# A gate projection as seven products of halves: layer 1 of a hybrid decoder trunk on one Trainium2 core

## The chip, the core and the metric

The kernel runs on one core of a Trainium2 chip. The core has TensorE (PE, matmuls; its weight loads are listed as PEld), VectorE (DVE), ScalarE (ACT), GpSimd (POOL) and SyncE (SP, which here only issues transfers). The metric is the device time of one run in microseconds; lower is better. Before the change the median of three runs is 888.65 us (888.0 to 889.33).

## The reference

Two layers over x of 1024 tokens and 1024 features, all in float32. Layer 0 is sliding-window attention, layer 1 a gated linear recurrence (HGRN2). Both end with a gate z, an output projection, a norm and a residual. The change touches layer 1 and the end of layer 0:

```python
def hgrn2_mixer(h, lower_bound, w_in, gnorm_w, w_out):
    proj = h @ w_in                                   # 1024 x 4096
    q, f, i, z = jnp.split(proj, [1024, 2048, 3072], axis=-1)
    q = silu(q); log_f = ...; k = -expm1(log_f); v = i   # 8 heads, key and value width 128
    o = chunked_gated_recurrence(q, k, v, log_f)      # S_new = S * decay + k^T v, head by head
    o = o * rsqrt(mean(o * o) + eps) * gnorm_w
    o = o.reshape(B, T, 1024) * silu(z)
    return o @ w_out

for layer in range(2):
    h = rmsnorm(x, pre_norm_w[layer])
    y = mixer(h)
    x = x + rmsnorm(y, post_norm_w[layer])
```

The gate projection z = h @ W_z is a product of 1024x1024 by 1024x1024.

## The kernel before

**Products.** float32 operands are split into a high and a low part (float32r): the high part is a rounded copy, the low part the difference. `product` (L230) then issues three matmuls of 128x512 for one block: high by high, high by low, low by high. Weights come as a stream of 128x512 entries, 256 KB each (list `SRC`). `fetch` issues their transfers on SP into four raw slots in turn (L151); for each entry `advance` issues a high split on ScalarE (L187) and a low split on VectorE (L188) into one of ten pairs of buffers (`whi`, `wlo`). An entry is split when a pair is free, and a raw slot is fetched again when its low split is done. Activations lie transposed and split in `act[k, half]` (k the eight blocks of 128 features, half the tokens 0 to 511 or 512 to 1023).

**Layer 0's end.** `output0` runs the output projection of layer 0, the norms and the residual row by row, and for each half of the tokens transposes the normed rows into `act[k, half]` (`transpose_half`, L289; high part on ScalarE at L212, low part on VectorE at L218).

**Layer 1.** `mixer1` runs a list of units, `plan`: units of i (value projection, columns 0 to 511 as c = 0 and 512 to 1023 as c = 1), of q and f (`qf`, one head), and `rec(h)`, the recurrence of head h. In `rec`, VectorE prepares two scans U and V (L973, L974) and products of them, TensorE makes the scores (psd L1004, pss L1014, psq L1030), transposes the keys (pst L1047), ScalarE copies them to `yn` (L1048), TensorE forms the chunks' updates (psk L1053), VectorE chains the state S through seven chunks (L1057, L1059), and TensorE reads it for the output (pso L1066, L1068), which is normed into `vo` (L1074). `yn` and `S` have one buffer each. Between the units of i stand four rounds of `weight_sums` (L1087 to L1090), each of which loads four blocks of the output projection's weights into the buffers of `yn` and `S`, forms sums of quarters there on VectorE and stores them to DRAM (`td`).

The gate z is 16 units of 24 matmuls (eight feature blocks by three): two of them ahead of `rec(7)`, six after, eight in `final1`. Each is evicted by a Sigmoid on ScalarE (L1106), a product on VectorE (L1107) and a product with the recurrence's output on GpSimd (L1108). `final1` then has the output projection in seven products of quarter matrices in place of eight (Strassen's scheme in Winograd's form): each takes four row blocks of 12 matmuls, and reads sums of quarters of both operands.

**The order.** The instructions of each engine have a fixed order, made when the kernel is built: a scheduler places units that the code gives with priorities (`hp()` raises the splits) and marks (`keep_in_program_order`). An engine takes its instructions one after the other, so one that waits holds those behind it. The program holds two variants of the network and chooses by the data; the runs here take the first.

Of the kernel before, what the change touches and what calls it, by code (L numbers as in the profile page):

```python
# [23 lines left out]
P = 128  # L24
# [66 lines left out]
def emit(tc, I, out):  # L91
# [9 lines left out]
    with top:  # L101
# [10 lines left out]
        td = [dp.tile([4 * P, 512], F32, name=f"td{i}") for i in range(4)]  # L112
# [23 lines left out]
        B1 = 116  # L136
        SRC = [I["w"][i] for i in range(B1)]
        quarter = lambda q: [I["w"][B1 + 4 * q + k] for k in range(4)]
        sums_of = lambda i: [td[i][k * P:(k + 1) * P, :] for k in range(4)]
        SRC += quarter(0) + sums_of(0) + sums_of(1) + sums_of(2) + sums_of(3) + quarter(3) + quarter(1)  # L140
# [144 lines left out]
        def transpose_half(hns, half, scol, then={}):  # L285
            for k in range(NK):
# [3 lines left out]
                ins = act_from_psum(k, half, pt, cst[:, scol + k:scol + k + 1])  # L290
# [549 lines left out]
        def output0(o, fp):  # L840
# [21 lines left out]
            def norm(t):  # L862
                xn = xns.pop(t)
                hn = fp.tile([P, D], F32, tag="hn", bufs=5, name="hn")
                jk = fp.tile([P, D], F32, tag="jkx", name="jkx")
# [16 lines left out]
        def mixer1(fast, vo, rp):  # L882
# [8 lines left out]
            nb3 = 3 if fast else 2  # L891
# [187 lines left out]
            zu = [lambda t=t: z_unit(rp, vo, 0, t) for t in range(8)]  # L1079

            def weight_sums(k):
# [3 lines left out]
                for q, x in enumerate((b11, b21, b12, b22)):  # L1085
                    nc.sync.dma_start(x, I["w"][B1 + 4 * q + k])
                v.tensor_tensor(b22, b22, b12, op=ALU.subtract)  # L1087
# [22 lines left out]
        def final1(vo, fp):  # L1110


            wpost = fp.tile([P, D], F32, name="wpost1")
            nc.sync.dma_start(wpost, I["bc"][2:3, :].to_broadcast([P, D]))
            ssall = fp.tile([P, 2, 9], F32, name="ssall")

            af = {(k, 0): fp.tile([P, 512], F32, name=f"af{k}") for k in range(NK)}
            af.update({(k, 1): vo[k // 4][:, k % 4, :] for k in range(NK)})
            late = [vo[k // 4][:, 4 + k % 4, :] for k in range(NK)]
            s3 = late[:4]  # L1120
            s2p = [(fp.tile([P, 512], F32R, name=f"s2h{k}"), fp.tile([P, 512], F32R, name=f"s2l{k}")) for k in range(4)]
            p1 = [fp.tile([P, 512], F32, name=f"p1_{t}") for t in range(4)]
            u3 = [fp.tile([P, 512], F32, name=f"u3_{t}") for t in range(4)]
# [14 lines left out]
            def part(ps, left, e, t, more, done=True, cols=(0, 512)):  # L1138

                c = slice(t * P, (t + 1) * P)  # L1140
                for k in range(4):
                    hi, lo = left[k]
                    product(ps, k, (hi[:, c], lo[:, c]), weight(e, k, *cols), None if more else 0, 3)
                    if done:
                        used(e + k)

            def row_part(c, t, y, x, cs, ss):

                jk = fp.tile([P, 512], F32, tag="sg", bufs=2, name="jk")
                nc.scalar.activation(jk[:, :cs.stop - cs.start], y, AF.Square, scale=D ** -0.5, accum_out=ss)  # L1150
# [229 lines left out]
```

## Time and profile before

| | |
|---|---|
| median of three runs | 888.65 us (888.0 to 889.33) |
| the profiled execution: its time, its span | 888.05 us, 886.3 us |
| granted TensorE clock | 0.998 |
| busy: PE, DVE, ACT, POOL | 98%, 68%, 48%, 38% |
| matmul records | 5214 |
| stage of layer 0's last transposes | about 360 to 402 us |
| sums of the output projection's weights | 402 to 437 us |
| z, with rec(7) in it | 690 to 800 us |
| out projection | to 878 us |

The page's section 1 gives busy time and share of each engine, section 4 the chain of work that ended last. The timeline gives start, duration, engine, line and operation of single instructions, with the idle time before them and what ended it in brackets. The windows give the busy time of each engine in a stretch, then clock, DMA share and GB/s. The list of waits gives for each line what it waited for: us in total, times, longest.

### The profile page before, as it was taken

To read this page: it belongs to the slowest core of one execution; us is meant where nothing else is said; L and a number is where in the kernel's file an instruction comes from. 1 tells how busy PE (TensorE), PEld (TensorE's weight loads), DVE (VectorE), ACT (ScalarE), POOL (GpSimd) and SP (SyncE) were. 2 spreads that over 40 slices of the span, in tenths; PEclk is the share of its full clock that TensorE was granted. 3 is DMA by queue.
4 is the path that set the end of the run, shared out by engine and by line. 5 is a ranking of instruction groups with operands and counts; after the bars stand their busy time and mean duration, and the time that the engine had idled before them with its cause. 6 is when DMAs were issued, how large, how long until landed. Compare 5 with 4: busy or idle time off the path is not lost.

```text
span 886.3 us, 14409 instructions
## 1 busy us (share of the span) xinstructions
PE 867.1 (98%) x5214; PEld 721.1 (81%) x5214; DVE 604.0 (68%) x975; ACT 426.9 (48%) x1094; POOL 333.0 (38%) x491
## 2 busy tenths in 40 slices
PE   6999999999999999999999999999999999999996
PEld 5887888888888878878888888888888788888885
DVE  6998887677899436764568775137668844448985
ACT  5735777767688332542323341343343333447432
POOL 4543644655666303320054342115243533220032
PEclk9999999999999999999999999999999999999999
DMA  9766455313232134555711010021111001503434
GB/s 339 274 204 176 145 167 154 92 50 96 58 92 85 48 89 149 170 177 192 264 51 40 27 49 1 20 89 36 48 50 36 13 1 51 187 1 107 131 123 167
DMA packets 61977, 94.17 MB, mean 106 GB/s; under 512 B 5832, under 2 KB 25928, under 8 KB 61896
## 3 DMA queue, kind: packets, MB, share of 16 engines
q1 hardware_dynamic: 61616, 93.08, 33.3%
q8 instruction: 43, 0.70, 0.3%
q14 instruction: 38, 0.31, 0.1%
q10 hardware_dynamic: 280, 0.07, 0.0%
HBM read 70.22 MB, written 21.07 MB: 103 GB/s over the span
## 4 chain that ended last, share of the span: by engine, by line
PE 81%; DVE 7%; issue 4%; POOL 3%; ACT 2%; DMA 2%; DVEq 0%; POOLq 0%; ACTq 0%
PE psmm L230 47%; PE psmm L88 20%; PE pss L88 3%; PE pso L88 2%; POOL rstd L269 2%; PE psk L1053 1%; PE pst L88 1%; PE pso L1066 1%; PE pso L1068 1%; POOL ms L267 1%; PE pst L1047 1%; PE pst L1134 1%; PE psd L1004 1%; DMA qd<-qh 1%; DMA out_dram<-xr 1%
## 5 line engine op out<-in xcount | busy, mean ns | idle before, releaser
L230 PE MATMUL psmm<-whi,acth 128*128 128x512 f32 x448 | 176.3, 395 | 1.1 <-DVE y L832 1.1
L230 PE MATMUL psmm<-wlo,acth 128*128 128x512 f32 x448 | 175.0, 391 | 0.0
L230 PE MATMUL psmm<-whi,actl 128*128 128x512 f32 x448 | 174.9, 392 | 0.0
L188 DVE TENSOR_TENSOR wlo<-wraw,whi 128x512 fp32r<-128x512 f32 x132 | 96.3, 742 | 71.2 <-ACT whi L187 67.5
L187 ACT ACTIVATE whi<-wraw 128x512 fp32r<-128x512 f32 x124 | 77.5, 631 | 94.9 <-PE psmm L230 72.6
L88 PE MATMUL psmm<-acth,whi 128*128 128x512 f32 x272 | 110.5, 406 | 1.7 <-ACT whi L88 1.7
L88 PE MATMUL psmm<-actl,whi 128*128 128x512 f32 x272 | 107.3, 394 | 0.2 <-DVE actl L88 0.2
L88 PE MATMUL psmm<-acth,wlo 128*128 128x512 f32 x272 | 107.4, 395 | 0.0
L230 PE MATMUL psmm<-acth,whi 128*128 128x512 f32 x256 | 101.1, 395 | 0.2 <-DVE qf L906 0.2
L230 PE MATMUL psmm<-acth,wlo 128*128 128x512 f32 x256 | 100.4, 392 | 0.0
L230 PE MATMUL psmm<-actl,whi 128*128 128x512 f32 x256 | 100.3, 392 | 0.0
L230 PEld LDWEIGHTS psmm<-whi,acth 128*128 128x128 f32 x448 | 84.1, 188 | 19.1 <-DVE y L832 1.9
L230 PEld LDWEIGHTS psmm<-whi,actl 128*128 128x128 f32 x448 | 84.1, 188 | 17.2
L230 PEld LDWEIGHTS psmm<-wlo,acth 128*128 128x128 f32 x448 | 84.2, 188 | 16.7
L717 ACT ACTIVATE sm<-sm,st 128x129 f32<-128x129 f32 x128 | 49.9, 393 | 26.6 <-DVE st L715 26.5
L914 POOL TENSOR_SCALAR gate<-gate,lbt 128x512 f32<-128x512 f32 x16 | 17.8, 1109 | 118.9 <-ACT gate L912 108.4
L88 PEld LDWEIGHTS psmm<-acth,wlo 128*128 128x128 f32 x272 | 51.6, 190 | 11.7 <-DVE wlo L88 0.2
L88 PEld LDWEIGHTS psmm<-acth,whi 128*128 128x128 f32 x272 | 51.8, 191 | 10.3 <-ACT whi L88 2.0
L88 PEld LDWEIGHTS psmm<-actl,whi 128*128 128x128 f32 x272 | 51.8, 190 | 8.6 <-DVE actl L88 0.7
L230 PEld LDWEIGHTS psmm<-acth,whi 128*128 128x128 f32 x256 | 48.1, 188 | 10.8 <-DVE qf L906 0.9
L230 PEld LDWEIGHTS psmm<-acth,wlo 128*128 128x128 f32 x256 | 48.1, 188 | 10.1
L230 PEld LDWEIGHTS psmm<-actl,whi 128*128 128x128 f32 x256 | 48.1, 188 | 9.4
(312 smaller groups left out, 1727.4 us busy)
## 6 DMA issues: line engine op xcount, KB each, us to landing
wraw<-in_w SPq DMA_DIRECT2D x128, 256.0 KB
QS<-qd SPq DMA_DIRECT2D x16, 512.0 KB
xr<-in_x SPq DMA_DIRECT2D x8, 512.0 KB
x1d<-xn SPq DMA_DIRECT2D x8, 512.0 KB
bq<-in_w SPq DMA_DIRECT2D x16, 256.0 KB
td<-bq SPq DMA_DIRECT2D x16, 256.0 KB
wraw<-td SPq DMA_DIRECT2D x16, 256.0 KB
xr<-x1d SPq DMA_DIRECT2D x8, 512.0 KB
```

What stands on the lines that cost most here:

```text
L88: return (lambda *a, **k: self.tc.keep_in_program_order(f(*a, **k))) if self.on else f
L187: nc.scalar.activation(hi, raw, AF.Copy)
L188: W["split_ins"][i] = v.tensor_tensor(lo, raw, hi.bitcast(F32), op=ALU.subtract)
L230: W["mm"] = pe.matmul(ps, a, b, start=(k == first and i == 0), stop=(k == last and i == 2), skip_group_check=first is None)
L267: keep(g.tensor_scalar(m, ms, eps, 1.0, op0=ALU.add, op1=ALU.mult))
L269: W["rstd"] = keep(g.tensor_tensor(r, m, nhalf[:, :width], op=ALU.pow))
L717: W["exp"] = nc.scalar.activation(sm[:, h, :], sm[:, h, :], AF.Exp, bias=nm[:, h:h + 1], scale=-1.0, accum_out=dn[:, h:h + 1])
L914: nc.gpsimd.tensor_scalar(dst, dst, ol, lb, op0=ALU.mult, op1=ALU.add)
L1004: nc.tensor.matmul(ps[o:o + 32, c, :], V[:, cs], U[:, cs], start=True, stop=True)
L1047: nc.tensor.transpose(pt[:, i, :], Y[:, c * P:(c + 1) * P], ident)
L1053: nc.tensor.matmul(pk[:, i, :], yn[:, c, :], vt[:, c, hc], start=True, stop=True)
L1066: nc.tensor.matmul(po[:, i, :], sc[:, c, :], vt[:, c, hc], start=True, stop=(c == 0))
```

## The change

The gate projection of layer 1 is written as seven products of halves too (z1 to z7), so that both it and the output projection are. In numbers of matmuls, z goes from 16 x 24 = 384 to 7 x 4 x 12 = 336.

- The **sums of the inputs** (`zS1` to `zS4`, four sums of quarters of the normed, transposed activations) are formed in `output0` while the transposes lie in PSUM: 12 copies on ScalarE and 16 operations on VectorE more, and 16 stores of 256 KB to DRAM (`sd`). Later they come back as entries of the weight stream and are split into the buffers `act[k, half]` themselves. `INTO` says into which, and a counter `W["phase"]`, raised by `next_phase()`, holds the stream until the old contents have been read by the program.
- The **sums of the weights** are four more rounds of `weight_sums`, with its own quarters (`QZ`) and signs, between the units of i with c = 1; they go to DRAM (`tz`).
- The stream has 44 entries of 256 KB for z in place of 16 (28 of weights and weight sums, 16 of input sums).
- Of z's products, three row blocks of z1 stand ahead of `rec(7)`; the rest is in `final1` in the order z1, z7, z6, z4, z5, z3, z2. Their results are added on VectorE in SBUF, Silu on ScalarE is applied to the sum (in place of Sigmoid and a product), and GpSimd multiplies as before.
- The out projection's products come in another order of quarters (o1, o7, o6, o4, o5, o3, o2), and the pool of the recurrence stays open to the end; `final1` takes its buffers by name from those of the recurrence. Four buffers for the residual's rows in place of five.

```diff
+        for e in (("z1", QZ[0]), ("zS3", sd[0], (1, 1)), ("z7", tz[0]), ("zS2", sd[1], (0, 2)), ("z6", tz[1]), ("z4", tz[2]),
+                  ("zS1", sd[2], (1, 3)), ("z5", tz[3]), ("zS4", sd[3], (0, 4)), ("z3", QZ[3]), ("z2", QZ[2]),
+                  ("o1", QO[0]), ("o7", td[0]), ("o6", td[1]), ("o4", td[2]), ("o5", td[3]), ("o3", QO[3]), ("o2", QO[2])):
+            entries(*e)
...
+                elif i in INTO:
+                    k, half, phase = INTO[i]
+                    if W["phase"] < phase:
+                        return
+                    W["place"][i] = act[k, half]
...
+            def sums(k, half, pt, scale):
+                a1, a2 = vo1[:, k % 4, :], vo1[:, 4 + k % 4, :]
+                r = slice(k % 4 * P, k % 4 * P + P)
+                if half == 0:
+                    nc.scalar.activation(a1 if k < 4 else a2, pt, AF.Copy, scale=scale)
+                elif k < 4:
+                    a21[k] = fp.tile([P, 512], F32, tag="a21", bufs=2, name="a21")
+                    nc.scalar.activation(a21[k], pt, AF.Copy, scale=scale)
+                    v.tensor_tensor(a1, a21[k], a1, op=ALU.subtract)
+                    nc.sync.dma_start(sd[0][r], a1)
+                else:
+                    s2, s1 = fp.tile([P, 512], F32, tag="s2", bufs=2, name="s2"), a21[k - 4]
+                    v.scalar_tensor_tensor(s2, pt, scale, a1, op0=ALU.mult, op1=ALU.add)
+                    v.scalar_tensor_tensor(s1, pt, scale, s1, op0=ALU.mult, op1=ALU.add)
+                    v.tensor_tensor(a2, a2, s2, op=ALU.subtract)
+                    for d, x in ((1, s2), (2, s1), (3, a2)):
+                        nc.sync.dma_start(sd[d][r], x)
...
-            plan += qf(0) + ([zeros] if fast else []) + qf(1) + rc(0) + qf(2) + rc(1) + qf(3) + rc(2) + iu(1) + rc(3)
-            plan += qf(4) + qf(5) + rc(4) + qf(6) + rc(5) + qf(7) + rc(6) + zu[:2] + rc(7) + zu[2:]
+            def first_parts():
+                next_phase()
+                for t in range(3):
+                    first_part(t, p1z[t])
...
+            plan = ... rc(2) + with_sums(iu(1), QZ, tz, True) + rc(3)
+            plan += qf(4) + qf(5) + rc(4) + qf(6) + rc(5) + qf(7) + rc(6) + [first_parts] + rc(7)
...
-        def z_unit(pool, vo, c, t):
-            ps = proj_nat(100 + 8 * c, t)
-            sg = pool.tile([P, 512], F32, tag="sg", bufs=2, name="sg")
-            nc.scalar.activation(sg, ps, AF.Sigmoid)
-            v.tensor_tensor(sg, ps, sg, op=ALU.mult)
-            nc.gpsimd.tensor_tensor(vo[c][:, t, :], vo[c][:, t, :], sg, op=ALU.mult)
+            def gate(c, t, z):
+                nc.scalar.activation(z, z, AF.Silu)
+                nc.gpsimd.tensor_tensor(vo[c][:, t, :], vo[c][:, t, :], z, op=ALU.mult)
...
+            first_part(3, p1z[3])
+            next_phase()
+            for t in range(4):
+                ps = mm()
+                part(ps, quad(0, 1), "z7", t, False)
+                nc.scalar.activation(u3[t], ps, AF.Copy)
+            next_phase()
+            for t in range(4):
+                ps = mm()
+                part(ps, quad(0, 0), "z6", t, False)
+                v.tensor_tensor(p1[t], ps, p1z[t], op=ALU.add)
+                v.tensor_tensor(u3[t], u3[t], p1[t], op=ALU.add)
+            next_phase()
+            for t in range(4):
+                ps = mm(tag="to"[t % 2])
+                part(ps, quad(4, 1), "z4", t, False)
+                sg = sgs[t % 2]
+                v.tensor_tensor(sg, ps, u3[t], op=ALU.add)
+                gate(0, 4 + t, sg)
...
```

The line numbers from here on with another range are those of the changed kernel: its splits are L203 and L204, the copy of yn is L1088, the steps of S are L1097 and L1099, and the copy of F is L1009.

**ScalarE, around rec(6)'s copy of yn.** `sg` are z's sigmoids, `sc0` and `sc1` the masked scores of rec(6) and rec(7), `pst` the transposed keys. Before:

```order
L1106 ACTIVATE sg_6967<-psmm_6942 128x512 [waits DVE_49,PE_49]
L1033 ACTIVATE sc0_4153<-psq_6847 64x4x64 [waits PE_49]
L1033 ACTIVATE sc0_4153<-psq_6847 64x4x64
L1106 ACTIVATE sg_6996<-psmm_6971 128x512 [waits DVE_49,PE_49]
L1048 ACTIVATE yn_6868<-pst_6870 128x512 [waits PE_49]
L1048 ACTIVATE yn_6868<-pst_6885 128x512 [waits PE_49]
L1017 ACTIVATE sc1_4154<-pss_7058 32x4x32 [waits PE_49]
```

After (`acth0_0` to `acth3_0` take the sum zS2, `whi4` to `whi7` the weights of z6, `pair` are results of z1 and z7):

```order
L1073 ACTIVATE sc0_4219<-psq_6951 64x4x64
L203 ACTIVATE acth0_0_116<-wraw0_112 128x512 [waits DMAHW6_49,PE_49]
L203 ACTIVATE acth1_0_120<-wraw1_113 128x512 [waits DMAHW7_49,PE_49]
L203 ACTIVATE acth2_0_124<-wraw2_114 128x512 [waits DMAHW0_49,PE_49]
L203 ACTIVATE acth3_0_128<-wraw3_115 128x512 [waits DMAHW1_49,PE_49]
L1175 ACTIVATE pair_7288<-psmm_7301 128x512 [waits DVE_49,PE_49]
L203 ACTIVATE whi4_96<-wraw0_112 128x512 [waits DMAHW4_49]
L203 ACTIVATE whi5_97<-wraw1_113 128x512 [waits DMAHW5_49]
L1246 ACTIVATE pair_7288<-psmm_7345 128x512 [waits PE_49]
L1088 ACTIVATE yn_6972<-pst_6974 128x512 [waits PE_49]
L203 ACTIVATE whi6_98<-wraw2_114 128x512 [waits DMAHW6_49]
L1088 ACTIVATE yn_6972<-pst_6989 128x512 [waits PE_49]
```

No split stood ahead of the copy of yn between the two score copies before; now six splits do, two of which refill slots that the sum zS2 has just left, and a seventh stands between its halves.

**VectorE, around rec(5)'s state S.** Before:

```order
L188 TENSOR_TENSOR wlo4_98<-wraw0_104,whi4_88 128x512 [waits DMAHW2_49,PE_49,Activation_49]
L1057 COPY S_6565<-psk_6572 128x128 [waits PE_49]
L1059 SCALAR_TENSOR_TENSOR S_6565<-S_6565,tt_6470,psk_6572 128x128 [waits DVE_49] x3
L1059 SCALAR_TENSOR_TENSOR S_6565<-S_6565,tt_6470,psk_6587 128x128 [waits DVE_49,PE_49]
L1059 SCALAR_TENSOR_TENSOR S_6565<-S_6565,tt_6470,psk_6587 128x128 [waits DVE_49] x2
L188 TENSOR_TENSOR wlo5_99<-wraw1_105,whi5_89 128x512 [waits DMAHW3_49,PE_49,Activation_49]
L969 COPY F1_4155<-gate1_4158 128x64 [waits Pool_49]
```

After (`wlo2`, `wlo3`, `wlo8`, `wlo9` are weights of z7):

```order
L204 TENSOR_TENSOR actl3_1_131<-wraw3_115,acth3_1_130 128x512 [waits DMAHW1_49,Activation_49]
L1097 COPY S_6681<-psk_6688 128x128 [waits PE_49]
L1099 SCALAR_TENSOR_TENSOR S_6681<-S_6681,tt_6586,psk_6688 128x128 [waits DVE_49]
L204 TENSOR_TENSOR wlo2_104<-wraw0_112,whi2_94 128x512 [waits DMAHW2_49,Activation_49]
L1099 SCALAR_TENSOR_TENSOR S_6681<-S_6681,tt_6586,psk_6688 128x128 [waits DVE_49]
L204 TENSOR_TENSOR wlo3_105<-wraw1_113,whi3_95 128x512 [waits DMAHW3_49,Activation_49]
L1099 SCALAR_TENSOR_TENSOR S_6681<-S_6681,tt_6586,psk_6688 128x128 [waits DVE_49]
L204 TENSOR_TENSOR wlo8_110<-wraw2_114,whi8_100 128x512 [waits DMAHW4_49,Activation_49]
L1099 SCALAR_TENSOR_TENSOR S_6681<-S_6681,tt_6586,psk_6703 128x128 [waits DVE_49,PE_49]
L204 TENSOR_TENSOR wlo9_111<-wraw3_115,whi9_101 128x512 [waits DMAHW5_49,Activation_49]
L1009 COPY F1_4221<-gate1_4224 128x64 [waits Pool_49]
L1099 SCALAR_TENSOR_TENSOR S_6681<-S_6681,tt_6586,psk_6703 128x128 [waits DVE_49]
```

Six steps in a row before; now four low splits stand between them, and the copy of F ahead of the last.

**VectorE, between rec(6)'s scores and its state.** These are the rows from the last piece of rec(7)'s preparation (`tt_7120`) on, after the change:

```order
L1062 TENSOR_TENSOR qf_6481<-qf_6481,tt_6878 128x8x64 [waits PE_49]
L1030 TENSOR_TENSOR tt_7120<-tt_7120 128x8 [waits DVE_49]
L204 TENSOR_TENSOR actl0_0_117<-wraw0_112,acth0_0_116 128x512 [waits DMAHW6_49,PE_49,Activation_49]
L204 TENSOR_TENSOR actl1_0_121<-wraw1_113,acth1_0_120 128x512 [waits DMAHW7_49,PE_49,Activation_49]
L204 TENSOR_TENSOR actl2_0_125<-wraw2_114,acth2_0_124 128x512 [waits DMAHW0_49,PE_49,Activation_49]
L204 TENSOR_TENSOR actl3_0_129<-wraw3_115,acth3_0_128 128x512 [waits DMAHW1_49,PE_49,Activation_49]
L204 TENSOR_TENSOR wlo4_106<-wraw0_112,whi4_96 128x512 [waits DMAHW4_49,Activation_49]
```

The four low splits of zS2, which free the raw slots, stand behind the whole preparation of rec(7); before, there was no such sum, and z's weights came through slots that were free in time.

More of the change, by code (lines that the diff above doesn't have):

```diff
@@ L134, in emit, with entries @@
         wraw = [wp.tile([P, 512], F32, name=f"wraw{i}") for i in range(NR)]
[L136 to L140, printed above, removed]
+        QZ, QO = (100, 108, 104, 112), (120, 128, 116, 124)
+        SRC, INTO, E = [I["w"][i] for i in range(100)], {}, {}
+        def entries(name, src, into=None):
+            E[name] = len(SRC)
+            for k in range(4):
+                if into is not None:
+                    INTO[len(SRC)] = (k, *into)
+                SRC.append(I["w"][src + k] if isinstance(src, int) else src[k * P:(k + 1) * P, :])
+        for e in (("z1", QZ[0]), ("zS3", sd[0], (1, 1)), ("z7", tz[0]), ("zS2", sd[1], (0, 2)), ("z6", tz[1]), ("z4", tz[2]),
+                  ("zS1", sd[2], (1, 3)), ("z5", tz[3]), ("zS4", sd[3], (0, 4)), ("z3", QZ[3]), ("z2", QZ[2]),
+                  ("o1", QO[0]), ("o7", td[0]), ("o6", td[1]), ("o4", td[2]), ("o5", td[3]), ("o3", QO[3]), ("o2", QO[2])):
+            entries(*e)
         NS = len(SRC)
         W_K = 10
-        W = {"pos": 0, "bank": 0, "plan": [], "split": 0, "fetch": 0, "left": {}, "place": {}, "dmas": {}, "split_ins": {}, "free": list(zip(whi, wlo))}
+        W = {"phase": 0, "pos": 0, "bank": 0, "plan": [], "split": 0, "fetch": 0, "left": {}, "place": {}, "dmas": {}, "split_ins": {}, "free": list(zip(whi, wlo))}
         FIRST = (0, 2, 1, 3)
@@ L283, in norm_rows, with transpose_half @@
             return hn
-        def transpose_half(hns, half, scol, then={}):
-            for k in range(NK):
+        def transpose_half(hns, half, scol, then={}, order=range(NK), more=None):
+            for k in order:
                 pt = pp.tile([P, 512], F32, tag="tso"[k % 3], name="pst")
@@ L289, in transpose_half @@
                     nc.tensor.transpose(pt[:, j * P:(j + 1) * P], hns[j][:, k * P:(k + 1) * P], ident)
[L290 removed]
+                with hp() if more else ExitStack():
+                    ins = act_from_psum(k, half, pt, cst[:, scol + k:scol + k + 1])
+                if more:
+                    more(k, half, pt, cst[:, scol + k:scol + k + 1])
                 then.get(k, lambda: None)()
@@ L869, in norm @@
                 if t % 4 == 3:
-                    transpose_half(hns, t // 4, C_PRE + 8)
+                    transpose_half(hns, t // 4, C_PRE + 8, order=(0, 4, 1, 5, 2, 6, 3, 7), more=sums)
                     hns.clear()
@@ new lines, in mixer1, with next_phase, part, quad @@
+            return [rp.tile([P, D], F32, tag="sc", bufs=2, name="xr") for i in range(2)]
+        def next_phase():
+            W["phase"] += 1
+            advance()
+        def part(ps, left, e, t, more, cols=(0, 512)):
+            c = slice(t * P, (t + 1) * P)
+            for k in range(4):
+                hi, lo = left[k]
+                product(ps, k, (hi[:, c], lo[:, c]), weight(E[e], k, *cols), None if more else 0, 3)
+                used(E[e] + k)
+        def quad(k0, half):
+            return [act[k0 + k, half] for k in range(4)]
@@ L1136, in turned, with row_part @@
                     nc.scalar.activation(af[k, half], pt, AF.Copy, scale=cst[:, C_GN:C_GN + 1])
[L1138 to L1150, printed above, removed]
-                v.tensor_tensor(x, y, wpost[:, c * 512 + cs.start:c * 512 + cs.stop], op=ALU.mult)
+            def row_part(c, t, y, x, ss):
+                jk = sgs[t % 2]
+                nc.scalar.activation(jk, y, AF.Square, scale=D ** -0.5, accum_out=ss)
+                v.tensor_tensor(x, y, wpost[:, c * 512:(c + 1) * 512], op=ALU.mult)
             def add_eps(ss, eps):
@@ L1299, in arm @@
         def arm(fast):
-            W.update(split=0, fetch=NR, left={}, place={}, free=list(zip(whi, wlo)))
+            W.update(phase=0, split=0, fetch=NR, left={}, place={}, free=list(zip(whi, wlo)))
             network(fast)
```

181 lines of the change are left out of this document (98 added, 83 removed).

## The prediction, on record before the run

> **What bounds the kernel now.** I read the page first: busy shares, then the chain that ended last.
>
> ```profile
> span 886.3 us, 14409 instructions
> PE 867.1 (98%) x5214; PEld 721.1 (81%) x5214; DVE 604.0 (68%) x975; ACT 426.9 (48%) x1094; POOL 333.0 (38%) x491
> PE 81%; DVE 7%; issue 4%; POOL 3%; ACT 2%; DMA 2%; DVEq 0%; POOLq 0%; ACTq 0%
> ```
>
> TensorE is busy 98% of the span and carries 81% of the chain. Its waits, with the engine that ended them:
>
> ```profile
> PE psl L1293 <- DVE ld L1291: 4.9, 1, 4.9
> ...
> PE psd L1004 <- DVE tt L990: 1.3, 1, 1.3
> PE psmm L230 <- DVE y L832: 1.1, 2, 0.6
> ```
>
> After the wait at the start (4.9 us) none is over 2 us. The kernel is bound by the number of its matmuls; the other engines have just enough slack to keep out of the way. So two questions decide: how much TensorE work goes, and where the work added to the others makes TensorE wait.
>
> **1. What is removed.** The gate projection z takes 384 matmuls of 128x512 before (16 units of 24) and 336 after (7 products, each four row blocks of 12): 48 fewer. Their pitch is in the chain, in the z stage itself:
>
> ```profile
> 770.99 10.90 PE psmm L230 x48
> ...
> 789.13 10.90 PE psmm L230 x48
> ```
>
> 10.90 us for 48, or 0.227 each, gives **-10.9 us**. That is all that TensorE saves: the transposes and the recurrence are as before, and the out projection keeps its seven products.
>
> **2. The waits in the last two heads.** Here the change moves most. Rows of the timeline from rec(5)'s state to rec(6)'s output (S the state, psk its update, pso the output, psd and pss the chunk's scores, yn the transposed keys):
>
> ```profile
> 682.79 2.33 DVE L1059 SCALAR_TENSOR_TENSOR S<-S,tt,psk 128x128 f32<-128x128 f32 x6
> 686.42 0.39 PE L1068 MATMUL pso<-S,qf 128*128 128x128 f32 x2
> 687.47 0.71 DVE L969 COPY F<-gate 128x64 f32<-128x64 f32 x1 [0.68 <-POOL gate L914]
> 690.29 0.50 PE L230 MATMUL psmm<-whi,acth 128*128 128x512 f32 x1
> ...
> 707.04 0.33 PE L1004 MATMUL psd<-U,V 128*32 128x32 f32 x14 [1.33 <-DVE tt L990]
> 707.51 0.15 DVE L990 TENSOR_TENSOR tt<-tt 128x8 f32<-128x8 f32 x1
> 707.99 1.09 ACT L1048 ACTIVATE yn<-pst 128x512 f32<-128x512 f32 x2 [5.04 <-PE pst L1047]
> 708.99 1.16 PE L1053 MATMUL psk<-vo,yn 128*128 128x128 f32 x8
> ...
> 717.04 0.60 PE L1066 MATMUL pso<-vo,sc 128*128 128x128 f32 x4
> ```
>
> The next rows give the time in which a raw weight slot turns round: the first of four low splits at L188 ends near 747.7, and the high split of the following entry in that slot starts at 750.39, released by its transfer. That makes 2.7 us from the end of a low split to the next high split.
>
> ```profile
> 747.03 3.60 DVE L188 TENSOR_TENSOR wlo<-wraw,whi 128x512 fp32r<-128x512 f32 x4
> 750.39 0.63 ACT L187 ACTIVATE whi<-wraw 128x512 fp32r<-128x512 f32 x1 [1.36 <-DMA wraw<-in_w]
> ```
>
> *rec(5).* VectorE's order now has the four low splits of the third input sum ahead of the six steps of S, then low splits of z7's weights between the steps, and the copy of F ahead of the last step. Those weights come through slots that are free only when the sum's low splits are done. F is there at 687.47 in the trace; with its 0.71 and a step of 0.37 (2.33 over 6, rounded) S is done near 688.6. The pso that reads it stood at 686.42, so it waits 2.2 us, less about 0.2 for psd matmuls now put ahead: z's first matmul moves from 690.29 to about 692.3. Bounds: 0, if weights and gate are early, and 4, if all four transfers come one after another.
>
> *rec(6).* TensorE now does 60 z matmuls ahead of rec(7)'s psd instead of 63, and so comes there near 707.0 (692.3, plus the 15.4 from 690.29 to the start of the old wait, less 0.7 for 3 matmuls); the old wait of 1.33 disappears in this, and nothing of the 2.0 is left but that 3 matmuls (0.7 us) are not yet done. Then ScalarE: its copy of yn stands behind the high splits of z6's first two weight entries and a copy of u3. Those entries' slots still hold the second input sum, whose low splits stand on VectorE behind the whole preparation of rec(7), which ends at 707.66 in the trace (L990). So: two low splits, 708.4 and 709.0; plus 2.7, high splits from 711.1 and 711.8; the second ends at 712.4, u3's copy at 713.0, the first yn copy at 713.5. TensorE's psk starts at 713.7, not 708.99, 4.7 later. With the 0.7 of undone z matmuls that is 5.4; nine pss ahead of psk and nine psq ahead of pso are work done early, some 0.4 each. I take **+4.6 us** for both heads. Bounds: 1, if the slots come free early enough that only the splits queue, and 8, if VectorE's preparation is itself 2 us late and the second yn copy, behind one more split, is waited for too. What stands behind the blocked copy on ScalarE is splits and rec(7)'s mask copy, which TensorE doesn't need for another 5 us.
>
> [...]
>
> **3. Sums of the weights.** The four rounds for z run between rec(2) and rec(3), in the buffers of yn and S. The same rounds are in the trace once, for the out projection:
>
> ```profile
> 402.21 0.68 DVE L1087 TENSOR_TENSOR bq<-bq 128x512 f32<-128x512 f32 x1
> 410.59 0.69 DVE L1087 TENSOR_TENSOR bq<-bq 128x512 f32<-128x512 f32 x1 [5.51 <-DMA bq<-in_w]
> 420.06 0.68 DVE L1087 TENSOR_TENSOR bq<-bq 128x512 f32<-128x512 f32 x1
> 433.37 1.03 DVE L1087 TENSOR_TENSOR bq<-bq 128x512 f32<-128x512 f32 x1 [4.30 <-DMA bq<-in_w]
> 400.00:420.00 20.00, 20.00 (x92) 16.54 (x91) 9.54 (x14) 5.39 (x9) 0.00 (x0) 1.00 0.56 196
> 420.00:440.00 20.00, 20.00 (x90) 16.57 (x89) 11.21 (x17) 7.73 (x12) 1.88 (x2) 1.00 0.86 292
> 560.00:600.00 40.00, 40.00 (x308) 33.09 (x307) 13.88 (x26) 13.47 (x26) 5.43 (x6) 1.00 0.22 67
> 559.50 0.69 DVE L1074 TENSOR_TENSOR o<-pso,rstd 128x512 f32<-128x512 f32 x1 [8.10 <-POOL rstd L269]
> 596.22 1.72 PE L1053 MATMUL psk<-o,yn 128*128 128x128 f32 x14
> ```
>
> A round takes 8.4, 9.5 and 13.3 us; the windows' last three columns are TensorE's clock, the DMA share and GB/s, and the long round falls where that share is 0.86. S comes free about when rec(2)'s output is read, 559.5. A load is like a slot's turn, 2.7, so VectorE's first step is at 562.2. With rounds of x us, the last one's four steps (2.9), store (2.7) and the first half of rec(3)'s yn copy (0.55) are done at 568.35 + 3x, and psk wants them at 596.22. At 8.4 there are 2.7 us to spare; at the mean, 10.4, TensorE waits 3.3; at 13.3, 12. DMA share is 0.22 there now and these rounds come alone, so I am near the short one: **+0.8 us**, bounds 0 and 12. SP, in order, also holds the weight fetches behind a round's loads; the weight pairs already split cover that, and 0.8 has it in.
>
> [...]
>
> **4. Sums of the inputs, in layer 0's end.**
>
> ```profile
> 360.00:380.00 20.00, 19.44 (x95) 15.65 (x94) 17.24 (x26) 12.93 (x25) 6.74 (x8) 1.00 0.49 157
> 380.00:400.00 20.00, 19.41 (x98) 15.92 (x97) 10.88 (x15) 9.15 (x17) 5.90 (x7) 1.00 0.54 173
> 464.99 0.80 PE psd L1004 x52
> 459.67 0.57 DVE L990 TENSOR_TENSOR tt<-tt 128x8 f32<-128x8 f32 x1
> ```
>
> Added are 12 ScalarE copies and 16 VectorE operations of about 0.7 us (8 and 11 us). VectorE had 28.1 of 40 us, so the stage fills it; what hides them are i units of the first row blocks, whose operands are ready, and the idle half of VectorE after 400. Taken at **0**, bounds 0 and 2 (a matmul that waits for a low half behind three such operations). The 16 stores of 256 KB, 4.2 MB, go through SP ahead of the out projection's rounds; at the 292 GB/s above that is 14 us, partly in gaps, so I shift the rounds by 10. They delay rec(0)'s preparation on VectorE by perhaps 4.4 us, which ended at 460.2 with psd at 464.99: slack 4.7. **+0.5 us**, bounds 0 and 4.
>
> **5. z to the out projection.**
>
> ```profile
> 720.00:760.00 40.00, 40.00 (x243) 34.10 (x243) 16.91 (x26) 17.31 (x49) 14.14 (x15) 1.00 0.22 64
> 760.00:800.00 40.00, 40.00 (x195) 33.36 (x194) 16.86 (x23) 16.79 (x30) 8.64 (x7) 1.00 0.19 73
> 800.00:840.00 40.00, 40.00 (x185) 32.88 (x184) 35.05 (x58) 25.29 (x47) 1.80 (x2) 1.00 0.44 127
> ```
>
> 28 more entries are streamed and split, about 18 us of ScalarE (0.63) and 19 of VectorE (0.69); 16 sigmoids and 16 products become 8 copies, 16 Silu and 24 sums: 5 us more on each. Both engines had 33 to 34 of the 80 us before 800, so they go to 55 to 60 of some 76 (336 matmuls): covered on average, with bursts at phase changes, where operands of the next product are split just before they are used, and at o1's. **+0.7 us**, bounds 0 and 4. The end after the last matmul is the same work in other buffers: 0.
>
> **Sum.** -10.9 + 4.6 + 0.8 + 0 + 0.5 + 0.7 = -4.3 us. The profiled run took 888.05 us with a span of 886.3, 0.6 under the median of the runs shown (888.65). So **883.7 us**.
>
> **The rivals.**
>
> A, the forecast: most of the gain stays, a wait at rec(6)'s yn takes nearly half. 881 to 886. Chance 0.48.
>
> B, the waits are hidden: term 2 at its lower bound of 1 and the rest at 0, -9.9 us, **878.2**. For it: TensorE waited almost nowhere in 886 us, and VectorE's order may run ahead of what I read from it. Against it: the splits stand in front of the copy. 0.17.
>
> C, the bursts eat the gain: terms 3, 4 and 5 at 1.6, 2 and 3 make -10.9 + 4.6 + 6.6 = +0.3, **888.4**. For it: VectorE at 35 of 40 us from 800 to 840, and 44 transfers in place of 16, each able to stop two engines; against it: a quarter of each engine stays free. 0.18.
>
> D, slower: the rounds of z's sums. If each takes 13.3 us, TensorE waits 12 us at rec(3)'s psk: -10.9 + 4.6 + 12 + 0.5 + 0.7 = +6.9, **895**. It decides from a round of 11.6 us: there the wait is 6.9 and the total 1.8 slower. For it: one round in three was over that; against it: DMA share 0.86 then, 0.22 here. 0.14.
>
> The other 0.03 is spread. A measurement of this kernel tells about 0.2%, 1.8 us, from no change: faster is under 886.3 to 886.9, by run or median. Faster: A, B and a tenth of C, 0.68; within: most of C, 0.16; slower: D and the tail of C, 0.16. The range from 877.8 to 889.6 leaves out D and little of B.
>
> **What would show it.** Right: 48 fewer matmuls, 5166 in place of 5214, with the last one about 4 us earlier; one wait of 3 to 7 us at psk behind yn near 710; no wait at psk near 596. B is right if psk near 710 has no wait; C if many waits under 2 us lie from 720 to 810; D if one long wait lies near 596 and VectorE's first steps of the rounds are over 11.6 us apart. I am wrong altogether if the pitch in z is not 0.227, or if a wait over 3 us stands where I named none.

## The result, and the profile after

| | before | after |
|---|---|---|
| median | 888.76 us (888.0 to 889.33, 4 runs) | 899.83 us (899.21 to 900.33, 4 runs) |
| ratio to before, 95% interval | | 1.0124 (1.0111 to 1.0137): slower |
| span of the profiled execution | 886.3 us | 898.4 us |
| granted TensorE clock | 0.998 | 0.986 |
| forecast | | 883.7 us (877.8 to 889.6) |

The kernel became about 11 us slower, where I had it 4 faster. The page's busy shares, the clock over the 40 slices and the chain by engine, after:

```profile
span 898.4 us, 14633 instructions
...
PE 863.6 (96%) x5166; PEld 716.6 (80%) x5166; DVE 642.4 (72%) x1043; ACT 453.6 (50%) x1143; POOL 343.8 (38%) x491
...
PEclk9999999999999999999999999999999989997999
...
PE 74%; DVE 9%; DMA 5%; ACT 4%; POOL 4%; issue 4%; SPq 0%; DVEq 0%; POOLq 0%; ACTq 0%
```

The 48 matmuls are gone (5166), yet TensorE is busy only 3.5 us less, and its share of the chain falls from 81% to 74%. Two slices of the clock row drop under 9. TensorE's waits (us in total, times, longest), after:

```profile
PE pst L1208 <- POOL o L1237: 7.7, 1, 7.7
PE psk L1093 <- ACT yn L1088: 5.4, 2, 4.8
PE psl L1385 <- DVE ld L1383: 5.3, 1, 5.3
PE psmm L246 <- DVE qf L946: 2.6, 2, 2.4
...
PE pso L1106 <- DVE S L1099: 1.4, 2, 1.0
```

The wait of 5.3 is the one at the start, as before. New are 7.7 for GpSimd at the first transposes of the out projection, 4.8 for the copy of `yn`, and 2.4 for the eviction of a q unit. Windows around the three (us, busy time of PE, PEld, DVE, ACT, POOL with counts, clock, DMA share, GB/s), after:

```profile
440.00:460.00 20.00, 17.59 (x70) 14.06 (x70) 12.56 (x16) 3.92 (x7) 7.00 (x10) 0.91 0.75 244
700.00:720.00 20.00, 15.23 (x177) 12.26 (x175) 18.28 (x25) 8.32 (x15) 8.03 (x5) 0.92 0.34 108
720.00:740.00 20.00, 20.00 (x146) 16.87 (x146) 11.77 (x22) 11.57 (x36) 5.00 (x6) 0.91 0.47 148
800.00:820.00 20.00, 13.61 (x66) 10.87 (x64) 20.00 (x32) 13.26 (x26) 13.85 (x2) 0.89 0.28 79
820.00:840.00 20.00, 18.74 (x75) 15.46 (x76) 11.79 (x20) 12.46 (x23) 1.20 (x1) 0.85 0.28 78
```

The same five windows of before all had clock 1.00. From 800 to 820 VectorE is busy for the whole 20 us, and GpSimd spends 13.85 us on two instructions. Finer windows show where the clock falls: it is 0.50 from 447.12 to 450.53, from 716.77 to 723.60 and from 815.76 to 826.00 us.

To place the loss I set the same point of both traces side by side (starts from the timeline; the last rows count the 128x512 matmuls that are left, and 336 of them are the out projection):

| point | before | after | lag |
|---|---|---|---|
| psd, rec(0) | 464.92 | 469.20 | +4.3 |
| psd, rec(3) | 576.75 | 580.99 | +4.2 |
| psk, rec(3) | 596.22 | 601.78 | +5.6 |
| psd, rec(5) | 655.29 | 660.60 | +5.3 |
| pso, rec(5) | 685.87 | 691.90 | +6.0 |
| psd, rec(7) | 707.04 | 712.18 | +5.1 |
| psk, rec(6) | 708.99 | 719.19 | +10.2 |
| pso, rec(6) | 717.04 | 729.31 | +12.3 |
| pso, rec(7) | 739.14 | 751.75 | +12.6 |
| 336 matmuls left | 800.00 | 801.78 | +1.8 |
| 288 left | 812.60 | 823.45 | +10.9 |
| 240 left | 823.48 | 835.57 | +12.1 |
| last matmul | 878.02 | 889.74 | +11.7 |

Between rec(7) and the out projection the lag shrinks by 10.8, which is the 10.9 of 48 matmuls less 0.1. So the gain is there in full, and 22.6 us were lost beside it: 4.3 ahead of rec(0), 1.0 by rec(5)'s start (1.3 at rec(3)'s psk, before a small part came back), 7.3 from there to rec(7), 0.1 over z and 9.9 in the out projection.

**The largest loss, at the out projection.** Rows of the timeline (start, duration, engine, line, operation, idle time before and its releaser), after:

```profile
800.73 1.34 POOL L1237 TENSOR_TENSOR o<-o,p1z 128x512 f32<-128x512 f32 x1 [3.25 <-ACT p1z L1236]
800.83 1.79 DVE L1308 TENSOR_TENSOR pair<-pair 128x512 f32<-128x512 f32 x1
807.36 0.68 DVE L204 TENSOR_TENSOR wlo<-wraw,whi 128x512 fp32r<-128x512 f32 x1
807.50 13.70 POOL L1237 TENSOR_TENSOR o<-o,pair 128x512 f32<-128x512 f32 x1 [5.42 <-ACT pair L1236]
807.96 0.68 DVE L1201 TENSOR_TENSOR actl<-vo,acth 128x512 fp32r<-128x512 f32 x1
...
819.40 0.68 DVE L204 TENSOR_TENSOR wlo<-wraw,whi 128x512 fp32r<-128x512 f32 x1
821.26 1.11 PE L1208 MATMUL pst<-cst,o 128*128 128x128 f32 x4 [7.65 <-POOL o L1237]
822.60 0.63 PE L246 MATMUL psmm<-wlo,acth 128*128 128x512 f32 x1
824.74 0.69 DVE L1201 TENSOR_TENSOR actl<-pair,acth 128x512 fp32r<-128x512 f32 x1 [4.66 <-ACT acth L1200]
```

GpSimd's product of the recurrence's output with the gate takes 1.34 us at 800.73 and 13.70 at 807.50. From 807.96 to 819.40 VectorE starts 20 operations 0.60 us apart without a gap, each a sum or difference of two SBUF tiles; the last ends at 820.08, and the product ends at 821.20, 1.12 later. TensorE waits 7.65 us for it, then runs nine matmuls of 128x512 0.43 us apart (their rows read 0.63), where 0.23 is usual (rows of 0.39). At 800.83 it is the other way round: GpSimd had begun first, and VectorE's operation took 1.79 in place of 0.68.

**The second loss, at rec(6).** Rows of the timeline, after:

```profile
713.34 0.16 DVE L1030 TENSOR_TENSOR tt<-tt 128x8 f32<-128x8 f32 x1
713.41 2.49 DVE L204 TENSOR_TENSOR actl<-wraw,acth 128x512 fp32r<-128x512 f32 x4
716.90 1.27 ACT L203 ACTIVATE whi<-wraw 128x512 fp32r<-128x512 f32 x2 [6.31 <-DMA wraw<-tz]
718.55 0.59 ACT L1088 ACTIVATE yn<-pst 128x512 f32<-128x512 f32 x1
719.19 2.08 PE L1093 MATMUL psk<-vo,yn 128*128 128x128 f32 x8 [4.77 <-ACT yn L1088]
```

ScalarE idles 6.31 us at a split that waits for its transfer, with the copy of `yn` behind it, and TensorE waits 4.77 for that copy. Its eight psk then take 2.08 us where before they took 1.16, at a clock of 0.50.

**The third, ahead of rec(0).** Rows of the timeline, after:

```profile
441.13 0.69 DVE L1129 TENSOR_TENSOR bq<-bq 128x512 f32<-128x512 f32 x1 [4.26 <-DMA bq<-in_w]
443.02 0.69 DVE L1130 TENSOR_TENSOR bq<-bq 128x512 f32<-128x512 f32 x1 [1.19 <-DMA bq<-in_w]
444.83 0.68 DVE L946 TENSOR_TENSOR qf<-psmm,sg 128x512 f32<-128x512 f32 x1
445.57 0.50 PE L246 MATMUL psmm<-acth,whi 128*128 128x512 f32 x1 [2.40 <-DVE qf L946]
447.86 0.63 PE L246 MATMUL psmm<-acth,wlo 128*128 128x512 f32 x1
```

VectorE waits for two loads of a round of the out projection's sums, and the eviction of a q unit stands behind the round. TensorE waits 2.40 for it, and from 447.12, some 1.5 us later, it runs 3.41 us at half clock, which loses 1.7. With 0.2 at another q unit's eviction this is the 4.3.

This third loss is not the same in every execution. Five of the kernels below (both on the gate product, both on rec(6), and the two repairs together) have the order of the changed kernel on all four engines up to 713 us. In their traces psd in rec(0) starts at 466.09 to 467.71, a lag of 1.2 to 2.8 in place of 4.3; TensorE's longest wait at a q eviction is 1.0 to 1.9 us, and no half clock follows. The other two losses come again in every trace in which they were not repaired: from rec(5)'s pso to rec(7)'s pso the lag grows by 6.5 to 7.7, in the out projection by 9.3 to 10.4.

### The profile page after: what moved, and what is told of

Its sections match the earlier page's. It is cut to its first block, busy times and chain, and to the rows that moved or that the text cites. A ratio compares the mean times of both kernels' runs of the same rounds, so it can differ in the third digit from the quotient of the medians.

```text
span 898.4 us, 14633 instructions
## 1 busy us (share of the span) xinstructions
PE 863.6 (96%) x5166; PEld 716.6 (80%) x5166; DVE 642.4 (72%) x1043; ACT 453.6 (50%) x1143; POOL 343.8 (38%) x491
## 4 chain that ended last, share of the span: by engine, by line
PE 74%; DVE 9%; DMA 5%; ACT 4%; POOL 4%; issue 4%; SPq 0%; DVEq 0%; POOLq 0%; ACTq 0%
PE psmm L246 43%; PE psmm L88 17%; PE pss L88 3%; PE pso L88 2%; PE pso L1106 2%; POOL o L1237 2%; DMA bq<-in_w 1%; PE psk L1093 1%; PE pst L88 1%; PE pso L1108 1%; POOL rstd L285 1%; DVE wlo L204 1%; DMA wraw<-tz 1%; ACT whi L203 1%; DMA tz<-bq 1%
## 5 line engine op out<-in xcount | busy, mean ns | idle before, releaser
L204 DVE TENSOR_TENSOR wlo<-wraw,whi 128x512 fp32r<-128x512 f32 x144 | 102.2, 724 | 51.8 <-ACT whi L203 46.9
L203 ACT ACTIVATE whi<-wraw 128x512 fp32r<-128x512 f32 x136 | 84.3, 628 | 90.5 <-PE psmm L246 57.9
L88 PEld LDWEIGHTS psmm<-acth,wlo 128*128 128x128 f32 x272 | 51.5, 190 | 11.7 <-DVE wlo L88 0.2
L246 PEld LDWEIGHTS psmm<-acth,wlo 128*128 128x128 f32 x256 | 48.5, 190 | 10.2
```

Of the source, the lines that this page charges most:

```text
L88: return (lambda *a, **k: self.tc.keep_in_program_order(f(*a, **k))) if self.on else f
L203: nc.scalar.activation(hi, raw, AF.Copy)
L204: W["split_ins"][i] = v.tensor_tensor(lo, raw, hi.bitcast(F32), op=ALU.subtract)
L246: W["mm"] = pe.matmul(ps, a, b, start=(k == first and i == 0), stop=(k == last and i == 2), skip_group_check=first is None)
```

## The experiments

The first question was the largest loss. Theory A: VectorE's stretch without a gap keeps GpSimd's product out. Rivals: that product is late for another reason, or TensorE would be held there by VectorE anyway.

### VectorE does that one product itself

```diff
-                nc.gpsimd.tensor_tensor(vo[c][:, t, :], vo[c][:, t, :], z, op=ALU.mult)
+                eng = v if (c, t) == (0, 3) else nc.gpsimd
+                eng.tensor_tensor(vo[c][:, t, :], vo[c][:, t, :], z, op=ALU.mult)
```

> Edit: of the 16 gate products on GpSimd the last one (first half of the columns, row block 3), which took 13.70 us in the changed kernel's trace while its fifteen fellows took 1.29 to 1.73, goes to VectorE; all else as changed. Theory A (GpSimd's product could not finish while VectorE ran without a gap from 797.8 to 820.1): on VectorE it takes 0.7 us about where VectorE stands at 812; TensorE's wait of 7.7 us at L1208 goes, and with it the slow clock behind it (windows 800 to 840 at 0.89 and 0.85, some 3 us): 888 to 891 us for 899.8. Theory B (VectorE itself is the bound of this stage, and the product was only the last in line): the product waits in VectorE's queue, and TensorE then waits for it or for the splits behind it: 894 to 898 us.

Measured: 890.99 us (889.14 to 892.15), ratio to before 1.0027 (1.0014 to 1.004), 8.8 us under the changed kernel. Waits of this kernel, at the same place and at `yn`:

```profile
PE psk L1093 <- ACT yn L1088: 5.3, 2, 4.9
...
PE psmm L246 <- ACT o L1210: 1.7, 1, 1.7
```

The 7.7 has become 1.7, though VectorE has an operation more, and the clock stays full there (1.00 from 800 to 820); the wait at `yn` is untouched.

### A pause for VectorE

The product stays on GpSimd; VectorE copies one element of its result, placed early, so that it must stop until the product is done.

```diff
+                if (c, t) == (0, 3):
+                    with tc.high_priority(offset=2000):
+                        v.tensor_copy(ssall[:1, 0, 8:9], vo[c][:1, t, :1])
```

> Edit: the product stays on GpSimd, but VectorE gets one more instruction, a copy of one element of the product's result, which stands in its order where it is at about 814 us and makes it stop there until GpSimd is done. Theory A (GpSimd is kept out while VectorE runs): the product ends 1 to 2 us after VectorE stops, so it lasts 7 to 8.5 us, not 13.7; TensorE's wait falls from 7.7 to 1.5 to 3 us, and the time to 892 to 896 us, though VectorE was stopped. Theory B (the product is slow by itself or for its operands): it still lasts 13.7 us, VectorE stands idle until 821, and the time is 900 to 905 us.

Measured: 890.65 us (889.45 to 892.64), ratio 1.0022 (1.0012 to 1.0031), 9.2 less than the changed kernel and better than expected. Rows of its timeline:

```profile
806.34 7.69 POOL L1237 TENSOR_TENSOR o<-o,pair 128x512 f32<-128x512 f32 x1 [5.42 <-ACT pair L1236]
812.22 0.68 DVE L1201 TENSOR_TENSOR actl<-vo,acth 128x512 fp32r<-128x512 f32 x1
814.06 0.14 DVE L1240 COPY ssall<-o 1x1 f32<-1x1 f32 x1 [1.16 <-POOL o L1237]
```

VectorE stops at 812.90 and the product ends at 814.03, 1.13 later: the same 1.1 us as in the changed kernel, 7 us sooner, because VectorE stops sooner. Here the product's time, 13.70 or 7.69 us, is set by when VectorE pauses. Making VectorE wait 1.16 us saved 9.2. Theory A holds; what in VectorE's operations keeps the product out, no run isolated.

### The stores of the input sums, on another queue

For the loss ahead of rec(0), the theory was that the 16 stores on SP delay the loads of the rounds behind them.

```diff
-                    nc.sync.dma_start(sd[0][r], a1)
+                    nc.scalar.dma_start(sd[0][r], a1)
...
-                        nc.sync.dma_start(sd[d][r], x)
+                        nc.scalar.dma_start(sd[d][r], x)
```

> Edit: the 16 stores of the input sums are issued from ScalarE's queue, not SP's. The changed kernel came to rec(0)'s psd 4.3 us late: the rounds of the out projection's sums ran 16 to 21 us later than before, and q's eviction on VectorE stood behind a round that waited for its loads (TensorE waits 2.4 us, then half clock). Theory A (SP's order: the rounds' loads stand behind the stores, which wait for VectorE): the rounds start 10 to 20 us earlier, the wait at q's eviction goes, psd is reached 3 to 4.3 us earlier: 895.5 to 897 us. Theory B (the load on the DMA engines and on VectorE is what delays the rounds): the rounds move by less than 5 us, and the time stays at 899 to 900.5, or is worse if ScalarE is held by the stores.

Measured: 900.21 us (898.21 to 901.41), ratio 1.0136 (1.0119 to 1.0153): no gain. The mask load ahead of the rounds still goes out at 407.79 (387.73 before, 409.84 after), and the rounds' first steps are at 419.29, 429.37, 439.77 and 449.44 (418.64, 431.27, 441.13 and 451.33 after). SP's order past the stores is not what delays the loads. In the list of waits of this kernel SP itself waits for a store before it issues the mask load:

```profile
SPq L928 <- DMA sd<-vo: 21.9, 1, 21.9
```

So the loads wait for the stores to land wherever these are issued; whether for a buffer or for a semaphore that both use, the list doesn't say. In this trace psd in rec(0) starts at 466.05, 3.15 sooner than in the changed kernel's, but that is the earliest of the five traces above (466.09), whose stores are on SP; and 3.4 us at half clock now follow a wait of 1.75 at rec(5)'s pso.

### No stores at all

```diff
-                    nc.sync.dma_start(sd[0][r], a1)
...
-                    for d, x in ((1, s2), (2, s1), (3, a2)):
-                        nc.sync.dma_start(sd[d][r], x)
```

> Edit: the 16 stores of the input sums are left out, and the entries that would read them read blocks of weights instead (same size and number; the gate is then not the reference's). The sums are still formed. Theory A (the out projection's rounds come late, because their loads stand on SP behind the stores, or because the stores load the DMA engines): the rounds' first loads are issued near 388 us as before and not at 410, VectorE's first step of a round comes 10 us or more earlier, TensorE's wait at q's eviction near 445 goes, psd of rec(0) is reached near 465.5 (469.2 in the changed kernel's trace, 464.9 before): 896 to 898 us. Theory B (the extra work on VectorE and ScalarE delays the rounds): loads still near 410, no gain, 899 to 900.5 us.

Measured: 898.41 us (897.05 to 898.7), ratio 1.0111 (1.0095 to 1.0126), 1.4 under the changed kernel. Rows of its timeline:

```profile
388.99 2.24 SPq L1124 DMA_DIRECT2D bq<-in_w  x4
408.33 0.69 DVE L1128 TENSOR_TENSOR bq<-bq 128x512 f32<-128x512 f32 x1
417.17 0.69 DVE L1129 TENSOR_TENSOR bq<-bq 128x512 f32<-128x512 f32 x1
438.84 0.69 DVE L1128 TENSOR_TENSOR bq<-bq 128x512 f32<-128x512 f32 x1 [5.23 <-DMA bq<-in_w]
442.95 0.68 DVE L945 TENSOR_TENSOR qf<-psmm,sg 128x512 f32<-128x512 f32 x1
```

The loads are back where they were before the change (388.99; before, 388.25), so the stores do delay them, on whichever queue they are issued. But the first round's second step comes 8.8 us after its first, the third round again starts only at 438.84 after 5.23 us for a load, and the q eviction still stands behind its steps (TensorE waits 1.3 us for it). By the medians only 1.4 us come back without the stores. In this trace psd in rec(0) starts at 465.67, as theory A had it; that is 3.5 sooner than in the changed kernel's trace, but only 0.4 sooner than the earliest of the five above. What is left would then be the place of the rounds in VectorE's order, which the last run changes.

### ScalarE's copy of yn ahead of z6's splits

For the loss at rec(6): the high splits of z6 are placed behind the copy of `yn`, ScalarE's order alone.

```diff
-                        nc.scalar.activation(hi, raw, AF.Copy)
+                        with tc.issue_after(W["yn", 6].ins) if E["z6"] <= i < E["z6"] + 4 else ExitStack():
+                            nc.scalar.activation(hi, raw, AF.Copy)
```

> Edit: on ScalarE alone the high splits of z6's weights stand behind rec(6)'s copies of yn; VectorE's order is left, with low splits of z6 and z4 ahead of and between the steps of rec(6)'s state. With both orders changed the time was 892.2. Theory A (the state's steps are held by the same transfers): the wait of 4.8 us at psk goes, but pso of rec(6) waits 3 to 5 us for S, and the slow clock stays: 897 to 900 us. Theory B (ScalarE's copy was the only thing held): 891.5 to 893.5 us.

Measured: 895.53 us (894.46 to 897.12), ratio 1.0083 (1.0068 to 1.0099), 4.3 less than the changed kernel. The wait of 4.8 is gone; the list of waits of this kernel has smaller ones in its place:

```profile
PE pso L1107 <- DVE S L1100: 2.7, 2, 1.6
...
PE psq L1071 <- DVE qf L1063: 1.1, 1, 1.1
```

VectorE is next: low splits of z6 stand between the steps of rec(6)'s S and wait there for their high splits. So 3.3 of the 7.6 us that the next run returns hide behind the first blocked copy.

### Both orders: splits of z6 and z4 behind yn and S

```diff
+                with (ExitStack() if W["plan"] else hp()), ExitStack() as held:
+                    if E["z6"] <= i < E["z4"] + 4:
+                        held.enter_context(tc.issue_after(W["yn", 6].ins))
+                        held.enter_context(tc.issue_after(W["S", 6].ins))
```

> Edit: on ScalarE the high splits of z6's and z4's weights stand behind rec(6)'s copies of yn, and on VectorE their low splits behind the last step of rec(6)'s state. Theory A (the copy of yn was late only because of the transfers that the splits ahead of it wait for): TensorE's wait of 4.8 us at psk goes, and with it the slow clock from 714 to 740 (about 2 us): 892 to 894.5 us. Theory B (the wait moves: z6's and z4's weights come later, and TensorE waits for them at z6 or z4): 897 to 900 us, with a new wait of 2 to 5 us for a split of the weights between 745 and 775.

Measured: 892.21 us (890.03 to 892.8), ratio 1.0043 (1.0027 to 1.006), 7.6 less than the changed kernel. From its waits:

```profile
PE pst L1211 <- POOL o L1240: 7.7, 1, 7.7
...
PE psk L1096 <- ACT yn L1091: 0.4, 1, 0.4
```

At `yn` 0.4 us is left, psk starts at 711.51 and pso at 719.93 (719.19 and 729.31 after the change); GpSimd's 7.7 is as it was. The queue order at rec(6) costs about 7.6.

### The two repairs together

The edit of the first kernel and the one just above in one.

> Edit: the last gate product on VectorE and, as in the run that held them, z6's and z4's splits behind rec(6)'s yn and state. Theory A (two separate waits, each with the slow clock behind it): the gains of the two runs add, 8.9 and 7.6 us from 899.8: 882.5 to 884.5 us, faster than the kernel before by 4 to 6 us. Theory B (VectorE is full from 798 to 830 in the changed kernel, and what comes to it earlier only waits longer there): 886 to 889 us.

Measured: 884.14 us (882.92 to 884.65), ratio 0.9946 (0.9932 to 0.9959): faster than before. 8.84 and 7.62 make 16.5, and 15.7 are measured, so the losses are separate and very nearly add.

### And the rest of the order

To these two, z7's splits are placed behind the last step of rec(5)'s S, and the out projection's rounds two to four stand later in the plan, the steps of the last two behind the evictions of q units on VectorE.

```diff
+                    if E["z7"] <= i < E["z7"] + 4:
+                        held.enter_context(tc.issue_after(W["S", 5].ins))
...
+                with tc.issue_after(W[behind].ins) if behind else ExitStack():
                     ... the round's four subtractions and additions
...
-            plan = plan[:1] + wo[:1] + plan[1:3] + wo[1:2] + plan[3:5] + wo[2:3] + plan[5:7] + wo[3:] + plan[7:] + qf(0) + ([zeros] if fast else []) + qf(1) + rc(0) + ...
+            plan = plan[:1] + wo[:1] + plan[1:4] + wo[1:2] + plan[4:] + q0[:3] + wo[2:3] + q0[3:] + ([zeros] if fast else []) + q1[:1] + wo[3:] + q1[1:] + rc(0) + ...
```

> Edit: as the run with both, and z7's low splits behind the last step of rec(5)'s state (a wait of 1.1 us of TensorE at pso), and rounds 2 to 4 of the out projection's sums later in the program, the last two on VectorE behind an eviction of q (waits of 0.9 to 2.4 us near 445). Theory A (these waits are on the path): 1 us and 1.5 to 3 us less than with both: 879 to 881.5 us. Theory B (the rounds now hold rec(0)'s preparation, or z7's splits come late): no gain over the run with both, or 1 to 2 us worse.

Measured: 880.23 us (879.9 to 881.26), ratio 0.9908 (0.9893 to 0.9923), 0.92% faster than before and the best of all. Its page:

```profile
PE 857.7 (98%) x5166; PEld 712.4 (81%) x5166; DVE 644.2 (73%) x1044; ACT 454.2 (52%) x1143; POOL 329.4 (37%) x490
```

Its waits in the out projection, at the evictions of q and at `yn`:

```profile
PE psmm L251 <- ACT o L1217: 1.7, 1, 1.7
...
PE psmm L251 <- DVE qf L951: 0.7, 2, 0.5
...
PE psk L1098 <- ACT yn L1093: 0.4, 1, 0.4
```

The span is 878.5 us and the clock 0.997. rec(0)'s psd starts at 464.87 (464.92 before), 1.2 sooner than in the earliest of the five traces above, so none of that loss is left with the stores still there; rec(6)'s psk at 709.08 (708.99 before). The run holds two edits that no run separates. Against the trace of the two repairs the lag is 2.6 less at rec(5)'s psd (2.1 for 4.7), which is the rounds' part or the spread between executions, and 4.3 less at rec(7)'s pso (1.0 for 5.3), so that 1.7 are left for z7's splits. The out projection starts 9.8 us sooner than before (790.20), and the last matmul 8.0 (870.04): of the 9.8, 1.8 are lost in the out projection, in this window of the same kernel:

```profile
800.00:820.00 20.00, 18.31 (x83) 14.95 (x83) 20.00 (x35) 15.50 (x29) 0.00 (x0) 1.00 0.36 95
```

VectorE is busy for all of it, at full clock; here its work itself seems to be the limit. That these 1.8 are VectorE's is read from this window and the 1.7 above; no run took work off it.

## Why the prediction was wrong

**What bounds the kernel, and term 1 (-10.9): right.** TensorE's matmuls set the time before, 48 fewer came, and the lag falls by 10.8 over z. With the waits ordered away the out projection begins 9.8 sooner than before.

**Term 2 (+4.6): the mechanism and place right, the size low.** The wait at psk behind `yn` is 4.77, where 4.7 was forecast; ScalarE's copy stood behind splits that waited for a transfer (6.31 idle). At rec(5) the two waits at pso are 0.45 and 0.95, 1.4 in all, not 2.0. The lag from rec(5) to rec(7) is 7.3, and ordering the splits behind `yn` and S returned 7.6. What I had not priced is that TensorE ran at half clock (0.50) after that wait: 2.1 us by rec(6)'s pso.

**Term 3 (+0.8): right.** The rounds' first steps are 7.5, 8.5 and 11.9 us apart, rec(3)'s psk waits 0.6 and lags by 1.3, and rival D's 12 us are not there. The kernel is slower, as D had it, but for other reasons.

**Term 4 (+0.5, bounds 0 and 4): mis-sized, and the wrong place.** I had the rounds delay rec(0)'s preparation, behind which there was slack. The rounds, started 16 us later (418.64 against 402.21), instead fell among the q units, and their steps stood on VectorE ahead of a unit's eviction: 2.4 and 0.2 of wait and 1.7 of half clock, the 4.3 just over the bound, in this one trace (1.2 to 2.8 in five others). That the loads wait for the 16 stores was right, though not for SP's order: on another queue they waited all the same. Putting the rounds later took the loss away; leaving the stores out returned only 1.4.

**Term 5 (+0.7, bounds 0 and 4): the step that failed.** It added up the work of each engine over 76 us and found it "covered on average". At the start of the out projection it is not spread: VectorE had 22 us without a gap, and GpSimd, whose products I counted as unchanged, could not run one beside it: 13.70 us in place of 1.3. From z to the last matmul the changed kernel lost 10.0 (0.1 over z, 9.9 in the out projection) where the term had 0.7, and taking this one product off GpSimd, or pausing VectorE for 1.16 us, returned 8.8 and 9.2.

**The clock: a term that was missing.** Each of the three waits was followed by matmuls at a granted clock of 0.50; I had every wait at its own length.

**The rivals.** A's wait was there, but beside two others. B's 878.2, every wait hidden, is nearly what the last kernel has with its order repaired (880.23). C, the bursts, named the stage, but as many waits under 2 us that "stop two engines", at 3 in all, not as one instruction of a third engine that starves. Its price, 888.4, is 11 short. That the kernel would be slower had 0.16. "A wait over 3 us stands where I named none" came true with the 7.7.

## What to carry to other kernels

Where a change moves work to an engine in bursts, read the fullest 20 us of that engine, not its mean over the stage, and ask which other engine must get an instruction through just then: a short pause there, or moving the one product, was worth 9 us. Price a long TensorE wait at more than its length: here waits of 2.40, 4.77 and 7.65 us were followed by half clock that cost 1.7, 2.1 and 2.4 us more, and so was one of 1.75 in one place, while one of 1.88 in another was not. Before giving up a saving of matmuls, look at what stands in an engine's order ahead of the copies and evictions that TensorE waits for: moving one product and reordering two groups of steps turned 1.24% slower into 0.92% faster.

## What the runs showed of the hardware

- A GpSimd product of two SBUF tiles of 128x512, 1.29 us with VectorE idle (at 793.47 after the change), took 13.70 us beside 20 VectorE operations 0.60 us apart (without the stores, and with the splits behind yn and S, TensorE waits 7.6 and 7.7 us for the same product), and 7.69 where VectorE was made to pause; both times it ended 1.1 us after VectorE stopped. When GpSimd began first, a VectorE operation took 1.79 in place of 0.68. Which of VectorE's operations keep GpSimd out was not separated.
- After the change, apart from the end of the run, where TensorE is done, the granted TensorE clock fell to 0.50 three times: from 447.12, 716.77 and 815.76 us on, for 3.41, 6.83 and 10.24 us. The starts lie whole multiples of 3.413 us apart (79 and 29 times), so the trace can be cut into pieces at these borders. TensorE had idled 1.86, 2.34 and 2.15 us of the piece just before. In the run with the stores on another queue it idled 1.75 us of a window of that length, and 3.41 us at 0.50 followed. Behind a wait of 1.70 (the two repairs), 1.69 (the last run) or 1.6 (the pause) the clock stayed full. So it did at the start of the changed kernel's run, where 3.04 us of a piece (3.39 to 6.80) were idle: the first 14 us are left out of this. Over the whole span the clock is 0.997 or 0.998 before, with the two repairs and in the last run, and 0.986 to 0.996 in the other seven. The windows below show three places: after the change a wait of 2.40, of which 1.86 fall into one piece; in the run with the stores on another queue a wait of 1.75, all in one piece; in the run with the two repairs a wait of 1.88, of which 0.85 fall into one window and 1.02 into the next. In the first two the clock falls, in the third it doesn't. After the change:

```profile
443.71:447.12 3.41, 1.55 (x7) 1.29 (x8) 3.41 (x6) 0.87 (x2) 2.92 (x2) 1.00 0.69 226
447.12:450.53 3.41, 3.41 (x10) 2.67 (x9) 0.62 (x1) 0.00 (x0) 3.41 (x5) 0.50 0.93 261
```

With the stores on another queue:

```profile
690.37:693.78 3.41, 1.66 (x46) 1.43 (x44) 2.05 (x5) 2.22 (x10) 2.62 (x5) 1.00 0.63 220
693.78:697.19 3.41, 3.41 (x47) 3.03 (x46) 0.94 (x3) 1.14 (x8) 1.01 (x2) 0.50 0.02 5
```

With the two repairs:

```profile
440.99:444.40 3.41, 2.56 (x12) 1.78 (x10) 1.89 (x4) 1.32 (x4) 0.00 (x0) 1.00 0.59 216
444.40:447.82 3.42, 2.40 (x10) 1.99 (x11) 3.19 (x5) 0.56 (x2) 3.24 (x3) 1.00 0.80 246
447.82:451.23 3.41, 3.41 (x17) 2.81 (x15) 0.32 (x1) 0.03 (x1) 2.92 (x6) 1.00 0.84 291
```

In these traces 1.75 us of idle time in one piece were enough for half clock, and a wait of 1.70 was not. The idle time is that of the profile, which models the ends of matmuls, and no run set the wait on purpose.
